# A hybrid decoder layer: the scores' first product with half the key columns, and the states' products placed right behind the scores

## The chip, the cores and the metric

The kernel runs on one core of one Trainium2 chip. The metric is the device time of one execution in microseconds (us). Before the change it is 824.81 us, the median of three runs (824.79 to 825.79 us). The differences in this case are small, so times are given to a hundredth.

## The reference

One layer with two token mixers side by side, then a gated feed-forward part, on 512 tokens of 1024 channels in float32. The change touches one of the mixers, the chunked gated linear attention with 4 heads, 128 key channels and 256 value channels per head, and chunks of 64 tokens:

```
b = jnp.cumsum(gk, axis=3)
q_dec = q * jnp.exp(b)
k_inv = k * jnp.exp(-b)
k_end = k * jnp.exp(b_last - b)
causal = jnp.tril(jnp.ones((GLA_CHUNK, GLA_CHUNK), dtype=bool))
att = jnp.einsum("bhnid,bhnjd->bhnij", q_dec, k_inv)
att = jnp.where(causal, att, 0.0)
o_intra = jnp.einsum("bhnij,bhnjv->bhniv", att, v)
kv_chunk = jnp.einsum("bhnjd,bhnjv->bhndv", k_end, v)
...
return dec[..., None] * state + kv, state
...
o_inter = jnp.einsum("bhnid,bhndv->bhniv", q_dec, s_prev)
o = o_intra + o_inter
```

`att` are the scores, `kv_chunk` the products from which the running state is made, and `o` adds what comes from the scores and what comes from the state.

## The kernel before

The kernel joins two chunks of 64 tokens into one block of 128, so a head has four blocks (`NT` = 4, the loop index `p`). Tiles are 128 partitions by 512 elements. Large projections are made in `col_tile`: eight steps of three matmuls each (lines 448, 449, 450, in a form of 32-bit floats that is split in a high and a low part), 24 matmuls with 512 moving columns. The attention's own small products are plain float32 matmuls, and each of these is two passes on TensorE in the profile, so 4 calls are 8 rows of the trace.

The loop at lines 1228 to 1244 runs five times and overlaps two heads. In one turn the order in the source is: decays and queries of the new head; `scores` of the head before (`old`), and inside it the gated outputs of the head before that; keys of the new head; `states` of `old`; one projection `gate_r`; `outputs` of `old`; a second `gate_r`. In the last turn there is no new head, and the projections are those of `gate_b`. The text below calls the four times that a head's scores are made the first to the fourth head.

What the steps do, with their lines:

- `scores` (1020): four transposes of the decayed keys into one PSUM bank (1024); a copy of that bank to SBUF as `kt` on ScalarE (1026); between them the other head's gated transposes (1080) and their VectorE work (1083); then, into one bank, eight products (1032 and 1033), two for each block `p`; then one predicated copy on VectorE (1034) that writes the allowed scores into the tile `att`, which was set to zero once at the start. The tile `k` of a block holds five stretches of 64 columns, and `flat(k, p, i)` takes two of them, 128 columns, as the stationary operand. Both products have 64 moving columns (queries). In 1032 the second half of the 128 key columns is the later chunk, which the queries of the earlier chunk may not see: `keep` masks it.
- `states` (1038): three products of `kt` with the values (1046), two in one PSUM bank and one in a second, each 256 columns wide; then one copy (1050) and two multiply-adds (1053) on VectorE.
- `outputs` (1056): products of `att` with the values (1065) and of the queries with the states (1067), squares on ScalarE (1069), a sum on VectorE (1071), a power on GpSimd (500), and the scaled outputs on ScalarE (1074).

PSUM has two sets of banks: `mm_bank` takes one of five, `ax_bank` one of three. A bank is given out again when its last reader is done. The transposes, the scores, the states and the outputs use the small set; projections and one half of the gated transposes use the large set.

The order on each engine is not written out in this part. A planner walks through the program with its own estimate of every instruction's time and gives each engine, whenever it is free, the instruction earliest in the source whose inputs are ready by that estimate. The order is then fixed: on the chip each engine takes its instructions in that order and waits where an input is late. Weights are read ahead: `weight` issues loads on SyncE's queue, splits an earlier weight into its parts on ScalarE (385, 387) and VectorE (390), and hands pieces of the convolution (782 on ScalarE, 786, 778, 800 to 804 on VectorE) to the engines, so that these stand between the head's own work on the same queues.

Of the kernel before, what the change touches and what calls it, by code (L numbers as in the profile page):

```python
# [17 lines left out]
P = 128  # L18
D = 1024
T = 512  # L20
NT = T // P
# [54 lines left out]
def trunk_layer(ctx: ExitStack, tc: tile.TileContext, a: dict, out: bass.AP):  # L76
    nc = tc.nc
# [23 lines left out]
    def nm(s):  # L101
        return f"{s}_{next(names)}"

    def heap(dt=F32):
        return hp.tile([P, T], dt, tag="h", name=nm("h"))
# [13 lines left out]
    def mm_bank():  # L119
        return ps.tile([P, T], F32, tag="mm", name=nm("mm"), bufs=5)  # L120

    def ax_bank():
        return ps.tile([P, T], F32, tag="ax", name=nm("ax"), bufs=3)
# [14 lines left out]
    keep = cp.tile([P, P], U8, name="keep")  # L138
    att = gp.tile([P, NT, P], F32, name="att")
# [268 lines left out]
    def weight(name, j, ahead=LOOK):  # L408
        assert order[used[0]] == (name, j)
        prefetch(1)  # L410
        used[0] += 1
        prefetch(ahead)
        share = {"two": 2.5, "w_glu": RATE + 0.75}.get(name, RATE)

        fill(share + (1.75 if order[min(len(ready), len(order)) - 1] in ADDED else 0))
        return ready[used[0] - 1]
# [35 lines left out]
    def col_tile(w, acts, acc=None, lo=0, hi=T, at={}, ks=range(KT)):  # L452

        if acc is None:
            acc = mm_bank()
        for k in ks:
            s = slice(k * P, (k + 1) * P)
            ah, al = acts[k]
            mm3(acc[:, lo:hi], (w[0][:, s], w[1][:, s]), (ah[:, lo:hi], al[:, lo:hi]), k == 0, k == KT - 1)
            if k in at:  # L460
                at[k]()
        return acc
# [89 lines left out]
    start = tc.manual_schedule(engines=START)  # L552
    start.__enter__()
    rows = tp.tile([P, P], F32, tag="gain", name=nm("rows"), bufs=1)[0:KT, :]
# [259 lines left out]
    for k in range(KT):  # L814
# [3 lines left out]
        pa = col_tile(weight("w_glu", 2 * k), acts1)  # L818
        c = heap()
# [104 lines left out]
    rows = slice(32, 32 + RANK)  # L924
# [9 lines left out]
    rows = slice(96, 96 + RANK)  # L934
# [24 lines left out]
    def gl(n, tag, bufs):  # L959
        return gp.tile([P, n], F32, tag=tag, name=nm(tag), bufs=bufs)  # L960
# [3 lines left out]
    C = 64  # L964
# [5 lines left out]
    def flat(t, p, i):  # L970
        return t[:, p, i : i + 2, :].rearrange("p c j -> p (c j)")
# [4 lines left out]
    class Head:  # L976
# [43 lines left out]
        def scores(self, between=None):  # L1020
            q, k = self.q, self.k
            pt = ax_bank()
            for p in range(NT):
                nc.tensor.transpose(pt[:, p * P : (p + 1) * P], flat(k, p, 3), ident)
            self.kt = gl(T, "kt", 1)
            nc.scalar.copy(self.kt, pt)
            if between:
                between()
            pa = ax_bank()
            for p in range(NT):  # L1030
                c = p * P
                nc.tensor.matmul(pa[:, c : c + C], flat(k, p, 0), q[:, p, 0, :], start=True, stop=True)  # L1032
                nc.tensor.matmul(pa[:, c + C : c + P], flat(k, p, 1), q[:, p, 2, :], start=True, stop=True)  # L1033
            nc.vector.copy_predicated(
                att, keep.unsqueeze(1).to_broadcast([P, NT, P]), pa.rearrange("p (a i) -> p a i", a=NT)
            )

        def states(self):

            self.s = [None]  # L1040
            kv = []
            for p in range(NT - 1):
                if p % 2 == 0:
                    pkv = ax_bank()
                kv.append(pkv[:, (p % 2) * DV : (p % 2 + 1) * DV])
                nc.tensor.matmul(kv[p], self.kt[:, p * P : (p + 1) * P], self.v(p), start=True, stop=True)  # L1046
            for p, half in enumerate(kv):
                new = gl(DV, "state", 3)
                if p == 0:
                    nc.vector.tensor_copy(new, half)  # L1050
                else:
                    dec = self.dec[:, p : p + 1]
                    nc.vector.scalar_tensor_tensor(new, self.s[p], dec, half, ALU.mult, ALU.add)
                self.s.append(new)
# [33 lines left out]
    def gate_r(m):  # L1088
        pr = col_tile(weight("w_r", m), acts1)
        sr[m] = heap()  # L1090
        nc.scalar.activation(sr[m], pr, AF.Silu)
# [3 lines left out]
    def gate_b(m):  # L1095
        gbs[m] = col_tile(weight("w_gb", m), acts1)
# [131 lines left out]
    for h in range(HEADS + 1):  # L1228
        old = heads[h - 1] if h else None
        new = heads[h] if h < HEADS else None  # L1230
        if new:
            new.decays()
            new.queries()
        else:
            gate_b(0)
        if old:
            old.scores(heads[h - 2].gated if h > 1 else None)
        new.keys() if new else gate_b(1)
        if old:
            old.states()  # L1240
        gate_r(2 * h) if new else gate_b(2)
        if old:
            old.outputs()
        gate_r(2 * h + 1) if new else gate_b(3)
# [378 lines left out]
    for gi, pairs in enumerate(GROUPS):  # L1623
        acts = []
        if gi == 0:
# [8 lines left out]
            p, q = pairs[0]  # L1634
# [139 lines left out]
```

## Time and profile before

| what | value |
|---|---|
| median of three runs | 824.81 us |
| the profiled execution: its time | 824.81 us |
| the profiled execution: span from first to last instruction | 823.1 us |
| mean granted TensorE clock | 0.998 of full speed |
| the attention's loop in the span | about 168 to 285 us |

How to read the rows of the trace: in the order of time, a row is the start in us, the time it took, the engine, the line, the operation, what it writes and reads, the operands' shapes and the number of instructions joined in the row; in brackets the idle time of the engine just before it and what ended it. PE is TensorE's matmul and PEld its weight load, which runs beside PE; DVE is VectorE, ACT is ScalarE, POOL is GpSimd. Matmuls are pipelined, so a row's length (from issue to the modelled end) is longer than the step to the next row, and the step is what counts for PE. The page's groups by line give a mean in ns and the idle time before.

### The profile page before, as it was taken

The numbers are of one execution on the slowest core, as the hardware profiler recorded it, in microseconds if no ns is written. First come the engines' busy times: TensorE is split into PE (matmuls) and PEld (weight loads), VectorE is DVE, ScalarE is ACT, GpSimd is POOL, SyncE is SP. The second block draws the span as 40 slices with busy tenths as digits, with TensorE's granted clock in tenths as the row PEclk, the third lists the DMA queues.
The fourth block names the chain that finished last, engine by engine and source line by source line (L and its number), as shares of the span: only waits on it lengthen the run. The fifth ranks groups of instructions, "written<-read, shape, count | busy, mean of one in ns | idle before, by whom it ended". The sixth has DMA issues, their size and how long they took to land.

```text
span 823.1 us, 11554 instructions
## 1 busy us (share of the span) xinstructions
PE 814.2 (99%) x4323; PEld 704.3 (86%) x4323; DVE 717.1 (87%) x1161; ACT 449.6 (55%) x666; POOL 149.6 (18%) x133
## 2 busy tenths in 40 slices
PE   8999999999999999999999999999999999999996
PEld 7888888888888889999988898898889988899885
DVE  6689999998989599886788889979975999789896
ACT  6643447656664446684454546556435653466654
POOL 2000010001100213543001000230123301612012
PEclk9999999999999999999999999999999999999999
DMA  8355672563433103323647623146632457234662
GB/s 318 102 130 144 148 192 87 129 154 103 101 105 103 51 30 124 104 78 113 203 117 220 192 77 103 32 170 159 140 136 83 142 138 165 105 103 166 167 129 103
DMA packets 30616, 106.27 MB, mean 129 GB/s; under 512 B 3464, under 2 KB 3600, under 8 KB 30560
## 3 DMA queue, kind: packets, MB, share of 16 engines
q1 hardware_dynamic: 24784, 85.34, 30.3%
q0 software_dynamic: 5760, 20.19, 14.4%
q8 instruction: 34, 0.56, 0.3%
q14 instruction: 22, 0.18, 0.1%
q10 hardware_dynamic: 16, 0.00, 0.0%
HBM read 103.42 MB, written 2.10 MB: 128 GB/s over the span
## 4 chain that ended last, share of the span: by engine, by line
PE 98%; DMA 1%; ACT 0%; DVE 0%; POOL 0%; issue 0%; POOLq 0%; SPq 0%; ACTq 0%
PE mm L448 28%; PE mm L449 28%; PE mm L450 28%; PE mm L662 3%; PE ax L450 2%; PE ax L449 2%; PE ax L448 2%; PE ax L1065 1%; PE ax L1067 1%; PE ax L1046 1%; DMA raw<-in_w_v_dram 1%; PE ax L1033 0%; PE ax L1032 0%; PE ax L529 0%; PE ax L576 0%; PE ax L1080 0%
## 5 line engine op out<-in xcount | busy, mean ns | idle before, releaser
L448 PE MATMUL mm<-uh,wlo 128*128 128x512 f32 (+1 forms) x672 | 244.4, 364 | 0.0
L449 PE MATMUL mm<-ul,whi 128*128 128x512 f32 (+1 forms) x672 | 242.3, 361 | 0.0
L450 PE MATMUL mm<-uh,whi 128*128 128x512 f32 (+1 forms) x672 | 242.0, 360 | 0.0
L450 PEld LDWEIGHTS mm<-uh,whi 128*128 128x128 f32 x672 | 126.8, 189 | 19.4
L448 PEld LDWEIGHTS mm<-uh,wlo 128*128 128x128 f32 x672 | 127.0, 189 | 18.9
L449 PEld LDWEIGHTS mm<-ul,whi 128*128 128x128 f32 x672 | 127.0, 189 | 18.6
L385 ACT CAST whi<-raw 128x1024 fp32r<-128x1024 f32 x86 | 89.8, 1047 | 59.9 <-PE mm L450 33.8
L356 DVE TENSOR_TENSOR wlo<-raw,whi 128x1024 fp32r<-128x1024 f32 x80 | 94.2, 1185 | 24.6 <-ACT whi L355 20.7
L327 POOL TENSOR_TENSOR raw<-raw,raw 128x512 f32<-128x512 f32 x42 | 67.5, 1608 | 212.8 <-DVE wlo L356 117.1
L390 DVE TENSOR_TENSOR wlo<-raw,whi 128x1024 fp32r<-128x1024 f32 x70 | 91.2, 1306 | 16.1 <-ACT whi L385 16.1
L355 ACT CAST whi<-raw 128x1024 fp32r<-128x1024 f32 x80 | 76.3, 957 | 35.9 <-PE mm L450 27.0
L786 DVE SCALAR_TENSOR_TENSOR c<-h,pp,c 128x255 f32<-128x255 f32 (+14 forms) x120 | 56.1, 467 | 3.7 <-ACT c L782 3.4
L786 DVE SCALAR_TENSOR_TENSOR c<-aside,btmp,c 128x255 f32<-128x255 f32 (+14 forms) x120 | 56.1, 467 | 2.8 <-ACT c L782 2.7
L786 DVE SCALAR_TENSOR_TENSOR aside<-h,pp,aside 128x255 f32<-128x255 f32 (+6 forms) x112 | 52.3, 467 | 0.0
L355 ACT CAST whi<-kept 128x1024 fp32r<-128x1024 f32 (+1 forms) x32 | 31.8, 995 | 30.6 <-DVE kept L310 17.1
L1498 DVE SCALAR_TENSOR_TENSOR tmp<-mm,pp,tmp 128x511 f32<-128x511 f32 (+1 forms) x56 | 41.4, 742 | 4.0 <-ACT tmp L1495 3.9
L356 DVE TENSOR_TENSOR wlo<-kept,whi 128x1024 fp32r<-128x1024 f32 (+1 forms) x32 | 36.8, 1153 | 4.8 <-ACT whi L355 4.7
L1176 ACT COPY tmp<-mm 128x256 f32<-128x256 f32 x48 | 17.6, 367 | 34.3 <-PE mm L450 33.9
L1414 DVE TENSOR_TENSOR hres<-hres,mm 128x512 f32<-128x512 f32 (+1 forms) x49 | 32.2, 670 | 4.2 <-PE mm L450 2.7
L1495 ACT ACTIVATE tmp<-mm,pp 128x512 f32<-128x512 f32 x28 | 21.8, 777 | 19.1 <-PE mm L450 18.9
L387 ACT ACTIVATE wlo<-raw 128x1024 fp32r<-128x1024 f32 x16 | 16.8, 1059 | 22.1 <-PE mm L448 22.1
L1498 DVE SCALAR_TENSOR_TENSOR tmp<-tmp,pp,tmp 128x511 f32<-128x511 f32 (+1 forms) x32 | 27.8, 888 | 0.4
(350 smaller groups left out, 1783.5 us busy)
## 6 DMA issues: line engine op xcount, KB each, us to landing
raw<-in_w_up_dram SPq DMA_DIRECT2D x44, 512.0 KB, 3.7
raw<-in_w_glu_dram SPq DMA_DIRECT2D x16, 512.0 KB, 4.8
raw<-in_w_down_dram SPq DMA_DIRECT2D x15, 512.0 KB, 4.1
kept<-in_w_down_dram POOLq DMA_DIRECT2D x10, 512.0 KB, 5.5
raw<-in_w_v_dram SPq DMA_DIRECT2D x8, 512.0 KB, 5.5
raw<-in_w_qk_dram SPq DMA_DIRECT2D x8, 512.0 KB, 3.3
raw<-in_w_r_dram SPq DMA_DIRECT2D x8, 512.0 KB, 4.6
wlo<-in_w_r_dram POOLq DMA_DIRECT2D x8, 512.0 KB, 8.0
```

The costliest lines, as they stand in the source:

```text
L327: work = nc.gpsimd.tensor_tensor(out, x, y, ALU.add)
L355: nc.scalar.copy(hi, raw)
L356: two_low[:] = [nc.vector.tensor_tensor(lo, raw, hi.bitcast(F32), ALU.subtract)]
L385: nc.scalar.copy(hi, raw)
L390: pace[0] = nc.vector.tensor_tensor(lo, raw, hi.bitcast(F32), ALU.subtract)
L448: nc.tensor.matmul(acc, ll, rh, start=first, stop=False, **kw)
L449: nc.tensor.matmul(acc, lh, rl, start=False, stop=False, **kw)
L450: nc.tensor.matmul(acc, lh, rh, start=False, stop=last, **kw)
L662: nc.tensor.matmul(acc, act, ready[k // 2][wi][:, j], start=first, stop=last)
L786: nc.vector.scalar_tensor_tensor(out[:, j:], x[:, : half_t - j], w, out[:, j:], ALU.mult, ALU.add)
L1414: done = nc.vector.tensor_tensor(hres[t, n][:, c], hres[t, n][:, c], acc[:, c], op)
L1498: nc.vector.scalar_tensor_tensor(z[:, s:], acc[:, : T - s], w[j], z[:, s:], ALU.mult, ALU.add)
```

## The change

- The two products of a block are no longer made one after the other. First all four blocks' first product, with 64 key columns as the stationary operand in place of 128, written to the first 64 partitions of the bank; then all four second products, as before.
- The masked copy into `att` becomes two: partitions 0 to 63 with all 128 columns of each block, and partitions 64 to 127 with the last 64 columns. The rest of `att` keeps the zeros of the start.
- In the loop, `states` moves from behind `keys` to right behind `scores`.
- Of the two PSUM banks of `states`, the second is taken from the large set.

```
             pa = ax_bank()
+            pb = pa.rearrange("p (a i) -> p a i", a=NT)
+
             for p in range(NT):
-                c = p * P
-                nc.tensor.matmul(pa[:, c : c + C], flat(k, p, 0), q[:, p, 0, :], start=True, stop=True)
-                nc.tensor.matmul(pa[:, c + C : c + P], flat(k, p, 1), q[:, p, 2, :], start=True, stop=True)
-            nc.vector.copy_predicated(
-                att, keep.unsqueeze(1).to_broadcast([P, NT, P]), pa.rearrange("p (a i) -> p a i", a=NT)
-            )
+                nc.tensor.matmul(pb[:C, p, :C], k[:, p, 0, :], q[:, p, 0, :], start=True, stop=True)
+            for p in range(NT):
+                nc.tensor.matmul(pb[:, p, C:], flat(k, p, 1), q[:, p, 2, :], start=True, stop=True)
+            for rows, cols in ((slice(0, C), slice(0, P)), (slice(C, P), slice(C, P))):
+                visible = keep[rows, cols].unsqueeze(1).to_broadcast([C, NT, cols.stop - cols.start])
+                nc.vector.copy_predicated(att[rows, :, cols], visible, pb[rows, :, cols])
...
                 if p % 2 == 0:
-                    pkv = ax_bank()
+                    pkv = mm_bank() if p else ax_bank()
...
             old.scores(heads[h - 2].gated if h > 1 else None)
+            old.states()
         new.keys() if new else gate_b(1)
-        if old:
-            old.states()
         gate_r(2 * h) if new else gate_b(2)
```

## The prediction

> **What bounds the kernel now.** I read the page first, then the busy time by stretch, then the timeline around each of the four places where a head's scores are made. The first five lines are the page's, the next two the busy time by stretch (start and end; then for each engine busy us and instructions; granted clock, DMA share, GB/s).
>
> ```profile
> span 823.1 us, 11554 instructions
> ...
> PE 814.2 (99%) x4323; PEld 704.3 (86%) x4323; DVE 717.1 (87%) x1161; ACT 449.6 (55%) x666; POOL 149.6 (18%) x133
> ...
> PE 98%; DMA 1%; ACT 0%; DVE 0%; POOL 0%; issue 0%; POOLq 0%; SPq 0%; ACTq 0%
> ```
>
> ```profile
> 176.00:203.00 27.00, 27.00 (x127) 22.63 (x126) 26.73 (x62) 13.40 (x24) 2.86 (x2) 1.00 0.49 124
> 168.00:300.00 132.00, 132.00 (x643) 111.77 (x643) 117.39 (x245) 72.82 (x125) 14.45 (x13) 1.00 0.36 96
> ```
>
> The reader is to see that TensorE is the bound, and in the attention's loop without any gap: busy 132.00 of 132.00 us. So a TensorE step that is saved there is won, and a wait that is put into its queue is lost in full. VectorE is nearly as full (117.39, and 26.73 of 27.00 between the first two heads' scores).
>
> The order of one turn, on the first head:
>
> ```profile
> 173.49 0.60 PE L1024 MATMUL ax<-ident,k 128*128 128x128 f32 x4
> 173.93 0.33 PE L1032 MATMUL ax<-q,k 128*128 128x64 f32 x2
> ...
> 175.64 0.47 PE L448 MATMUL mm<-uh,wlo 128*128 128x512 f32 x1
> ...
> 181.21 1.46 PE L1046 MATMUL ax<-h,kt 128*128 128x256 f32 x6
> ...
> 182.31 0.58 PE L448 MATMUL mm<-uh,wlo 128*128 128x512 f32 x1
> ...
> 184.72 0.68 DVE L1015 TENSOR_TENSOR k<-mm,tmp 128x512 f32<-128x512 f32 x1
> ```
>
> Transposes, scores (173.93 to 175.64: 1.71 us for 16 passes, 0.107 each), 5.6 us of keys, states, next projection: TensorE keeps the source's order. The keys stand between the transposes and the states, and that is the cover for the copy `kt` that the states read.
>
> **The copy `kt` against the end of the scores.** In each pair below one row is the weight load with which TensorE leaves the scores, the other ScalarE's copy, for the heads 1 to 4.
>
> ```profile
> 175.61 0.19 PEld L448 LDWEIGHTS mm<-uh,wlo 128*128 128x128 f32 x1
> ...
> 176.80 0.57 ACT L1026 COPY kt<-ax 128x512 f32<-128x512 f32 x1
> ...
> 204.89 0.19 PEld L448 LDWEIGHTS mm<-uh,wlo 128*128 128x128 f32 x1
> ...
> 207.41 0.58 ACT L1026 COPY kt<-ax 128x512 f32<-128x512 f32 x1
> ...
> 234.14 0.19 PEld L448 LDWEIGHTS mm<-uh,wlo 128*128 128x128 f32 x1
> ...
> 235.74 0.57 ACT L1026 COPY kt<-ax 128x512 f32<-128x512 f32 x1
> ...
> 261.56 0.58 ACT L1026 COPY kt<-ax 128x512 f32<-128x512 f32 x1
> ...
> 263.40 0.19 PEld L448 LDWEIGHTS mm<-uh,wlo 128*128 128x128 f32 x1
> ```
>
> The copy ends at 177.37, 207.99, 236.31 and 262.14: 1.76, 3.10 and 2.17 us after the scores in heads 1 to 3, and 1.26 before their end in head 4. Today nobody notices. With the states right behind the scores TensorE stands until the copy is there, and with it all that is queued behind: keys, both projections, the outputs.
>
> **What is late before the copy, and does it move?** For head 2, followed backwards from its outputs:
>
> ```profile
> 192.58 1.28 ACT L992 ACT_TABLE_LOAD   x1
> 194.25 1.22 DVE L990 TENSOR_TENSOR_SCAN b<-run,h 128x512 f32<-128x512 bf16 x1
> ...
> 195.50 0.64 ACT L992 ACTIVATE tmp<-b 128x512 f32<-128x512 f32 x1 [1.64 <-DVE b L990]
> 196.04 0.36 ACT L1069 ACTIVATE junk<-ax 128x256 bf16<-128x256 f32 x1
> ...
> 197.99 0.16 DVE L1071 TENSOR_SCALAR mean<-ss 128x4 f32<-128x4 f32 x1
> ...
> 198.24 2.00 POOL L500 TENSOR_TENSOR rstd<-mean,mhalf 128x4 f32<-128x4 f32 x1 [4.78 <-DVE mean L1071]
> ...
> 200.27 1.57 ACT L1074 ACTIVATE o<-ax,rstd 128x256 f32<-128x256 f32 x4 [2.77 <-POOL rstd L500]
> ```
>
> ScalarE takes `kt` behind the scaled outputs (1074), these wait for GpSimd's power, that for VectorE's sum (1071), that for the last square (1069), which stands on ScalarE behind an exponential (992) that waited 1.64 us for VectorE's scan (990). So it is VectorE's full queue that sets the time of head 2's copy, not TensorE. When TensorE loses 1.76 us in head 1, this chain does not follow: the squares before the table load move, but the load then ends at about 192.58 + 1.76 + 1.28 = 195.6, still when the scan is done. Heads 1 and 2 therefore do not add up: TensorE can't pass 207.99 whatever it lost before, a shift of **3.10 in all** by head 2.
>
> Head 3:
>
> ```profile
> 222.18 0.19 ACT L1069 ACTIVATION_READ_ACCUMULATOR junk<-ax 128x1 f32 x1
> ...
> 225.67 0.16 DVE L1071 TENSOR_SCALAR mean<-ss 128x4 f32<-128x4 f32 x1
> ```
>
> The sum came 3.30 after the last square, on VectorE's account again. TensorE and the squares 3.5 later use that up; the copy moves by some 0.8 (VectorE's added work, below) to 237.1, and the scores now end at 234.14 + 3.5 = 237.6 less what they save. No wait is left, barely. In head 4 the copy keeps its 1.26.
>
> **The change part by part.**
>
> *Half the key columns.* Eight of a head's 16 passes get 64 stationary columns for 128. No row has that shape. What the step of a pass hangs on, these rows tell:
>
> ```profile
> 337.09 0.95 PE L840 MATMUL ax<-ones,btmp 128*128 128x1 f32 x8
> 337.91 0.37 PE L448 MATMUL mm<-uh,wlo 128*128 128x256 f32 x1
> ...
> L1032 PE MATMUL ax<-q,k x32: 222/275/275, 173.9 to 263.1; 128*128 128x64 f32 x32
> ...
> L1034 DVE COPY_PREDICATED att<-keep,ax x4: 725/734/753, 178.7 to 264.3; 128x512 f32<-128x512 uint8 x4
> ...
> L1050 DVE COPY state<-ax x4: 415/416/418, 185.9 to 270.8; 128x256 f32<-128x256 f32 x4
> ```
>
> With one moving column the step is 0.82 / 8 = 0.1025, with 64 it is 0.107: moving columns hardly matter; it is the load of 128 columns, or a floor under each pass. If the load, halving saves 8 x 0.053 = 0.43 us a head; if a floor, nothing. Against that stands the change to another array shape and back, twice a head: if the array must first run empty, each costs a pass's length beyond its step, 0.275 - 0.107 = 0.17, so 0.34. The bounds are 0.43 saved and 0.34 lost; I take **0.25 saved**, since the step looks like a load and the drain may be partly hidden. In heads 1 and 2 it is worth nothing, for the copy sets the end there; in heads 3 and 4 it counts: 0.5.
>
> The Trainium skill, "TensorE: Matmul & The Clock Gate", section "LDWEIGHTS (loading the stationary operand)", has the load's time as columns over 1.2 GHz, 107 ns for 128 and 53 for 64. The step of 107 ns agrees for 128; by this rule alone an estimate of the sum below is 3.5 - 0.86 = 2.6. The Trainium skill, "TensorEngine Tiling (Array Packing)", section "Key Properties", says that a change of tiling mode, not just of tile, drains TensorE. It speaks against this change, no run here shows it, and with the drain at the price of the rows an estimate of the sum would be 3.5 - 2 x 0.09 = 3.3.
>
> *Two masked copies.* The first has the columns of today's (0.73 us), the second half of them, near the 0.416 of the 256-column copy: **0.4 us a head more on VectorE**. It is off TensorE's path, but ahead of the scan and the sum that lead to the next copy: head 2's moves from 207.99 to 208.4, and the shift from 3.1 to **3.5**. If the extra meets an idle stretch of VectorE it costs nothing.
>
> *States ahead of the keys.* Six passes move; none is added, and they issue no DMA. The weight loads and splits that the keys' call issues now follow three short VectorE operations (1050, 1053) in the source, on queues with a wait already. The keys come 1.1 us later, plus the wait; their reader on VectorE (1015) is at 184.72, 3.5 us after the keys' last product (before 181.21), which covers 1.1 + 1.76. If not, VectorE loses its lead and the second rival comes nearer.
>
> *A bank of the large set.* Head 2, with readers of three banks:
>
> ```profile
> 202.79 0.68 DVE L1008 SCALAR_TENSOR_TENSOR q<-mm,tmp 128x512 f32<-128x512 f32 x1
> 203.15 0.60 ACT L1091 ACTIVATE h<-mm 128x512 f32<-128x512 f32 x1
> ...
> 209.58 0.74 DVE L1083 SCALAR_TENSOR_TENSOR tmp<-ax,pp,h 128x512 f32<-128x512 f32 x1
> ```
>
> From the small set the third state product would have to wait for the gated half's reader, until 210.32. The large set's two last projections have been read by 203.75, before the scores end, so I cost this at nothing.
>
> **Sum.** 3.10 + 0.4 - 0.5 = **3.0 us**, on the profiled execution's 824.81 us (span 823.1 and 1.7 around it), which is the median: **827.8**. Its own range: 3.1 - 0.86 = 2.2 to 3.5 + 0.68 = 4.2, so 827.0 to 829.0.
>
> **The rivals.**
>
> *No wait (the other side).* The planner gives TensorE what its estimate holds ready. If it holds `kt` unready when the scores end, the keys go first and cover the copy; from 1.76 and 3.10 us of keys on (8 and 14 products of 0.23) the wait is gone, as it is if ScalarE takes the copy earlier. For it: head 4, where the copy is in time. Against: the copy follows the transposes by one instruction in the source, so an estimate without VectorE's lag has it ready. Then only the products count, four heads: from 1.7 faster to 1.4 slower, with 0.25 each 1.0 faster: 823.8.
>
> *Every head waits in full.* If the chain follows TensorE (VectorE's lead eaten up, or another order on ScalarE), the three gaps add up: 1.76 + 3.10 + 2.17 - 0.25 = 6.8, 831.6. Against it: head 2's chain above.
>
> *Narrow passes are dear.* If each waits for the one before (0.275 for 0.107), a head loses 8 x 0.168 + 0.34 = 1.7; head 1 hides it in its wait and head 2 too, heads 3 and 4 pay: 3.5 + 3.4 = 6.9, 831.7. Against it: loads run beside the products today.
>
> **How the numbers follow.** Forecast 0.59, no wait 0.24, every head in full 0.10, dear passes 0.07. The range 823.8 to 831.6 cuts about half of each rival, 0.20. From no change this measurement tells about 0.2%, 1.65 us. Faster by more needs no wait and nearly the whole 1.7: 0.09. Within: the rest of that rival, 0.15. Slower: 0.76.
>
> **What would show it.** TensorE idle before 1046, put down to ScalarE's 1026, some 2 us in head 1 and again in head 2, little or none in 3 and 4; first products with a step well under 0.107, perhaps a gap where their row begins and ends; a second masked copy of about 0.4; no idle time of VectorE before the second head's scan (990). Wrong: no idle before 1046 (then the order or the copy's place differs), or idle before it in head 3 as well.

## The result, and the profile after

The changed kernel takes 828.88 us (828.55 to 829.57, six runs) against 824.80 us (824.56 to 825.79, six runs) of the kernel before on the same chip: a ratio of 1.0046, interval 1.0035 to 1.0056. The forecast was 827.8 us, with a range of its own from 827.0 to 829.0 us.

The page of the changed kernel, its span and the engines' busy time; then TensorE's waits (what waited for what: us in all, times, the longest); then the busy time by stretch, in the columns of the prediction:

```profile
span 826.8 us, 11559 instructions
...
PE 816.6 (99%) x4323; PEld 705.8 (85%) x4323; DVE 720.2 (87%) x1165; ACT 450.0 (54%) x666; POOL 149.6 (18%) x133
```

```profile
PE ax L1048 <- ACT kt L1026: 2.1, 2, 1.6
PE mm L568 <- DVE ones L541: 1.1, 1, 1.1
```

```profile
168.00:303.70 135.70, 133.57 (x643) 111.89 (x642) 120.49 (x249) 73.06 (x125) 14.44 (x13) 0.99 0.36 94
...
175.00:178.00 3.00, 1.39 (x10) 1.20 (x9) 3.00 (x11) 2.05 (x3) 0.00 (x0) 1.00 0.97 172
178.00:181.00 3.00, 3.00 (x9) 2.39 (x8) 2.92 (x7) 0.00 (x0) 0.00 (x0) 0.50 0.69 218
181.00:184.00 3.00, 3.00 (x13) 2.40 (x12) 3.00 (x9) 0.00 (x0) 0.00 (x0) 0.93 0.03 11
184.00:187.00 3.00, 3.00 (x15) 2.48 (x14) 3.00 (x6) 0.93 (x1) 0.00 (x0) 1.00 0.00 0
```

The span grew by 3.7 us, from 823.1 to 826.8, and the attention's loop, which had no gap before, now has 135.70 - 133.57 = 2.13 us without TensorE: two waits for `kt`. That is not all of the 3.7. The rest stands in a column that was 1.00 throughout before: behind the first wait the granted clock is 0.50 for three microseconds and 0.93 for the next three, and TensorE does 9 and 13 instructions there instead of 15.

The timeline of TensorE behind the first head's scores shows both losses:

```profile
177.31 1.42 PE L1048 MATMUL ax<-h,kt 128*128 128x256 f32 x4 [1.61 <-ACT kt L1026]
178.52 1.06 PE L1048 MATMUL mm<-h,kt 128*128 128x256 f32 x2
...
180.23 0.63 PE L450 MATMUL mm<-uh,whi 128*128 128x512 f32 x1
180.66 0.63 PE L448 MATMUL mm<-uh,wlo 128*128 128x512 f32 x1
...
181.48 0.39 PE L450 MATMUL mm<-uh,whi 128*128 128x512 f32 x1
181.72 0.39 PE L448 MATMUL mm<-uh,wlo 128*128 128x512 f32 x1
```

After a wait of 1.61 us, products of 512 columns follow one another by 0.43 us (180.23 to 180.66) instead of 0.23, until about 181.4. The transposes of the second head, which stood at 201.90 before, stand at 205.20: 3.30 us later, of which 1.6 are the wait and 1.7 the half clock.

In the other heads, the same timeline shows the copy and then the states' products of heads 2, 3 and 4:

```profile
208.22 0.57 ACT L1026 COPY kt<-ax 128x512 f32<-128x512 f32 x1
...
208.84 1.13 PE L1048 MATMUL ax<-h,kt 128*128 128x256 f32 x4 [0.52 <-ACT kt L1026]
...
236.81 0.56 ACT L1026 COPY kt<-ax 128x512 f32<-128x512 f32 x1
...
238.03 1.08 PE L1048 MATMUL ax<-h,kt 128*128 128x256 f32 x4
...
265.37 0.58 ACT L1026 COPY kt<-ax 128x512 f32<-128x512 f32 x1
...
267.17 1.08 PE L1048 MATMUL ax<-h,kt 128*128 128x256 f32 x4
```

Head 2 waits 0.52 us, heads 3 and 4 not at all: their copies end at 237.37 and 265.95, 0.66 and 1.22 us before the states begin. From head 3 on nothing more is lost. Its transposes stand 3.93 us later than before (235.08 against 231.15), and the span ends 3.7 us later.

The scores themselves, first as pieces of the chain of waits (start, us, what), then rows of the timeline in stretches cut so that one or all eight passes are joined in a row, then the group of the masked copy:

```profile
236.55 0.61 PE ax L1033 x8
237.16 1.03 PE ax L1035 x8
238.19 0.92 PE ax L1048 x4
```

```profile
236.48 0.27 PE L1033 MATMUL ax<-q,k 128*64 128x64 f32 x1
...
236.48 0.68 PE L1033 MATMUL ax<-q,k 128*64 128x64 f32 x8
...
237.09 0.32 PE L1035 MATMUL ax<-q,k 128*128 128x64 f32 x1
...
237.09 1.10 PE L1035 MATMUL ax<-q,k 128*128 128x64 f32 x8
```

```profile
L1038 DVE COPY_PREDICATED att<-keep,ax x8: 445/581/732, 178.6 to 268.7; 64x512 f32<-64x512 uint8 x4, 64x256 f32<-64x256 uint8 x4
```

One pass alone takes 0.27, eight end after 0.68, so narrow passes follow by 0.41 / 7 = 0.058 us; for the wide ones it is 0.78 / 7 = 0.111. Half the columns is half the step. But eight narrow passes hold the chain for 0.61 us where 8 x 0.058 = 0.47, and eight wide ones for 1.03 where 8 x 0.111 = 0.89: some 0.15 us goes at each of the two changes of shape. Together the scores take 1.64 us (236.55 to 238.19) instead of 1.73 (in the chain before they went from 232.62 to 234.35): 0.09 us saved per head.

### The profile page after: what moved, and what is told of

It is laid out like the page before. It is cut to its first block, busy times and chain, and to the rows that moved or that the text cites. A ratio compares the mean times of both kernels' runs of the same rounds, so it can differ in the third digit from the quotient of the medians.

```text
span 826.8 us, 11559 instructions
## 1 busy us (share of the span) xinstructions
PE 816.6 (99%) x4323; PEld 705.8 (85%) x4323; DVE 720.2 (87%) x1165; ACT 450.0 (54%) x666; POOL 149.6 (18%) x133
## 4 chain that ended last, share of the span: by engine, by line
PE 76%; ACT 1%; POOL 0%; DVE 0%; issue 0%; POOLq 0%; ACTq 0%
PE mm L448 22%; PE mm L449 22%; PE mm L450 22%; PE ax L449 2%; PE ax L450 2%; PE ax L448 2%; PE ax L1067 1%; PE ax L1069 1%; PE ax L1048 1%; PE ax L529 0%; PE mm L1048 0%; PE ax L1035 0%; PE ax L1082 0%; ACT o L1076 0%; POOL rstd L500 0%; ACT L997 0%
```

## The experiments

All spans below are of the profiled execution and are compared with 823.1 us of the kernel before. "Waits" are TensorE's idle times before the states' products of heads 1, 2 and 3.

| kernel | waits, us | half clock in that execution | span | median, us (runs) | ratio to before |
|---|---|---|---|---|---|
| the whole change | 1.61, 0.52, 0 | after head 1 | +3.7 | 828.88 (6) | 1.0046 |
| half_only | none | no | -0.4 | 825.17 (11) | 0.9994 |
| move_only | 1.58, 0.67, 0 | no | +3.1 | 827.91 (5) | 1.0032 |
| head1_only | 1.61, 0, 0 | no | +1.8 | 828.23 (7) | 1.0029 |
| head1_fill | filled, 0, 0 | no | +1.5 | 826.79 (11) | 1.0019 |
| head2_only | 0, 2.28, 0 | after head 2 | +3.7 | 828.96 (5) | 1.0046 |
| in_keys2 | 0.22, 0.32, 0 | no | +0.5 | 825.58 (11) | 1.0004 |
| in_keys4 | none | no | -0.3 | 824.60 (11) | 0.9992 |
| all_fill1 | filled, 2.41, 0 | after head 2 | +5.6 | 831.07 (5) | 1.0071 |
| small_bank | 1.34, 0.64, 0 | no | +2.3 | 827.92 (9) | 1.0025 |
| all_fill12 | filled, 0.37, 1.95 | after head 3 | +7.8 | 833.25 (4) | 1.0090 |
| wide_keys4 | none | no | +0.4 | 825.93 (11) | 1.0006 |

The kernel before read 825.24 us on the chip of the first four experiments, 825.11 on that of the next four and 825.40 on that of the last three; the ratios go by these.

### One part alone: half_only and move_only

half_only is the changed kernel with the states put back:

```
             old.scores(heads[h - 2].gated if h > 1 else None)
-            old.states()
         new.keys() if new else gate_b(1)
+        if old:
+            old.states()
```

> The changed kernel with the states back behind the keys: half the key columns, grouped products, two masked copies and the bank of the large set stay. Theory (the whole loss is the wait for the copy kt and what TensorE's clock does after it): no idle before the states, a scores block of 1.64 us for 1.73, so 0.09 saved in each of four heads: 824.4. Rival A (the narrow array shape costs): 825.5 or more. Rival B (the second masked copy on VectorE delays the chain): up to 4 x 0.44 more, 826.5.

Measured: 825.17 us, ratio 0.9994 (0.9985 to 1.0002), no wait. The interval holds the 0.09 us x 4 = 0.36 us of gain that the chain shows (0.9996) and excludes the prediction's bound of 0.34 us lost in each head (1.0016) and both rivals (825.5 and 826.5 us at a before of 824.8, or 1.0008 and 1.0021).

move_only is the kernel before with the states moved and one bank from the large set, and the full-width products:

```
-                    pkv = ax_bank()
+                    pkv = mm_bank() if p else ax_bank()
...
             old.scores(heads[h - 2].gated if h > 1 else None)
+            old.states()
         new.keys() if new else gate_b(1)
-        if old:
-            old.states()
```

> The kernel before with only the states moved right behind the scores, their second bank from the large set; scores with 128 key columns and one masked copy. Theory: idle of about 1.7 us before the states of head 1, granted clock at half for some 3 us after it, a short idle in head 2, and 4 x 0.09 not saved: 828.9 to 829.3, no faster than the whole change. Rival A (narrow shape): 825. Rival B (second masked copy): 2 us under the whole change, about 827.

Measured: 827.91 us, ratio 1.0032 (1.0019 to 1.0045). At a before of 824.8 that is 827.4: 1.5 us under the theory and near rival B's 827. The profiled execution waits 1.58 and 0.67 us and keeps its clock; of its 3.1 us, 0.5 had come up before the first head (its transposes stand at 173.98 instead of 173.49). The two executions at clock 0.996 of the five (828.77 and 828.89) lie with the whole change. So the move alone carries most of the loss. A share of the second masked copy, by way of head 2's `kt`, is not excluded: with a single masked copy `kt` of head 2 ends at 207.97 here, and at 208.79 in the whole change, but the orders of VectorE and ScalarE differ as well. Without the move the second copy costs nothing that shows (half_only).

### The first head alone: head1_only and head1_fill

The states behind the scores in head 1, behind the keys in the others; then the same with TensorE kept busy by products of ones into a bank that nobody reads:

```
             old.scores(heads[h - 2].gated if h > 1 else None)
+            if h in (1,):
+                filler = mm_bank()
+                for _ in range(7):
+                    nc.tensor.matmul(filler[:, :P], ones, ones, start=True, stop=True)
-            old.states()
+                old.states()
         new.keys() if new else gate_b(1)
+        if old and h not in (1,):
+            old.states()
```

(head1_only is without the three lines of the filler.)

> The changed kernel with the states right behind the scores in head 1 alone, behind the keys in heads 2 to 4. Theory: 1.7 us of idle in head 1, then the clock at half for about 3 us, which costs 1.6 more; no other idle; 4 x 0.09 saved: 824.8 + 3.3 - 0.4 = 827.7. Rival (the clock costs nothing, heads 1 and 2 each pay their own wait): 824.8 + 1.7 - 0.4 = 826.1.

> As the run with head 1 alone, and ahead of head 1's states seven 128-column products of ones into a bank that nobody reads, 14 passes of 0.11 us, so that TensorE works through most of the wait. The wait itself stays. Theory: the clock stays at full, so 1.6 us come back: 826.1. Rival (the clock does not follow the idle): 827.7, as without the products.

Measured: 828.23 us and 826.79 us. The seven runs of head1_only spread over 2.5 us, and the mean granted clock of each sorts them in the main: four at 0.995 and 0.996 took 828.23 to 828.71 us, three at 0.997 to 0.999 took 826.25, 826.58 and 827.78. (By an estimate, some 3.4 us at half clock, as in the whole change, lower the mean over 825 us by 0.002.) The profiled run is the one of 826.58 us, and its stretch behind the wait shows the clock at full:

```profile
175.00:178.00 3.00, 1.39 (x10) 1.17 (x9) 3.00 (x11) 2.05 (x3) 0.00 (x0) 1.00 1.01 176
178.00:181.00 3.00, 3.00 (x15) 2.48 (x14) 2.92 (x8) 0.00 (x0) 0.00 (x0) 1.00 0.63 212
```

The same wait as in the whole change, 1.61 us, and 15 instructions behind it at full clock instead of 9 at half. This execution costs the wait alone, +1.8 us of span; the four at the lower clock have spans of 826.5 to 827.0, some 1.6 to 2.1 us more. With the filler all eleven runs read a clock of 0.997 or more, the wait's time stays lost, and the median falls by 1.4 us, though the intervals of the two ratios (1.0018 to 1.0041 and 1.0010 to 1.0028) overlap. So the half clock is a second loss behind a wait, in some executions and not in others. It is not the only spread: the run of 827.78 us has a clock of 0.999, and the kernel before reads 824.64 to 827.13 us on this chip at 0.997 to 0.999.

The prediction's claim that VectorE's queue, not TensorE, sets head 2's copy can be read in head1_only too (ScalarE's timeline):

```profile
194.12 1.28 ACT L992 ACT_TABLE_LOAD   x1
...
195.99 0.64 ACT L992 ACTIVATE tmp<-b 128x512 f32<-128x512 f32 x1 [0.58 <-DVE b L990]
...
207.91 0.57 ACT L1026 COPY kt<-ax 128x512 f32<-128x512 f32 x1
```

TensorE is 1.55 us late here (its second transposes stand at 203.45 instead of 201.90), and so is the table load; the exponential still waits 0.58 us for the scan, and the copy ends at 208.48, 0.49 us later than before. The scan and the sum stand at 194.73 and 198.48, 0.48 and 0.49 us later than before, so the whole shift is VectorE's. The forecast for that case was 208.4.

### The second head alone: head2_only

As head1_only, with `h in (2,)`.

> The changed kernel with the states' products right behind the scores in head 2 alone; heads 1, 3 and 4 as before, narrow first products everywhere. Times for a before of 824.8 us. If each head pays the whole distance from the end of its scores to its kt (the prediction's bound: in head 2 3.10 us before the change, and in the run with the narrow products alone kt ended 2.2 us after the scores), TensorE stands idle 2.2 to 3.5 us in head 2 and the time is 826.7 to 828.0 us, near the whole change without any wait in head 1, since the waits of heads 1 and 2 do not add up; up to 1.6 us more in executions in which the granted clock falls to a half after the wait. Rival (waits add up head by head, and head 2 costs only the 0.52 us that it shows in the whole change): 825.2 us.

Measured: 828.96 us, ratio 1.0046 (1.0032 to 1.0060): the whole change's time from one head. Its busy time by stretch:

```profile
205.00:208.00 3.00, 0.87 (x2) 0.79 (x3) 3.00 (x8) 3.00 (x6) 0.00 (x0) 0.83 0.00 0
208.00:211.00 3.00, 3.00 (x9) 2.38 (x9) 3.00 (x7) 3.00 (x6) 0.91 (x1) 0.60 0.58 178
```

The wait is 2.28 us and the half clock comes with it; with its 1.6 us the theory reaches the measured time. The rival (825.2 us) falls: what head 2 shows in the whole change, 0.52 us, is only what head 1 had not used up already. The wait is shorter than the 3.1 us of the prediction because the copy ends at 207.07 and not at 207.99: in this kernel's order VectorE takes the sum (1073) ahead of the next head's operations, as it does in half_only (at 196.99, against 197.99 before).

### Work put ahead of the wait: in_keys2, in_keys4, wide_keys4

The states go into the next key projection, behind 2 or 4 of its 8 steps (6 or 12 products of 512 columns):

```
-            old.states()
-        new.keys() if new else gate_b(1)
+        at = {1: old.states} if old else {}
+        new.keys(at) if new else gate_b(1, at)
```

(in_keys4 and wide_keys4 have `3` for `1`; `keys` and `gate_b` hand `at` on to `col_tile`, which calls it behind that step. wide_keys4 is the kernel before with this and with the bank of move_only.)

> The whole change, but the states' products stand behind the first 2 of the 8 steps of the next key projection (6 products of 512 columns, 1.36 us by 0.227 us each) instead of directly behind the scores. Theory (the wait is for kt's copy alone, so work put ahead shortens it one for one): idle before head 1's states 0.3 to 0.5 us instead of 1.61, before head 2's about 1.5 to 2; 826.3 to 827.0 us at a before of 824.8, and 1.6 us more where the clock falls after head 2's wait. Rival (the loss lies in the states' products themselves, their bank or the narrow products): as the whole change, 828.6 us.

> The same with 4 of the 8 key steps ahead (12 products, 2.72 us). Theory: no idle before head 1's states, 0 to 1 us before head 2's; 824.4 to 825.5 us at a before of 824.8. Rival: 828.6 us.

> The kernel before, with its full-width first products, but the states' products moved up to behind the fourth of the eight key steps and one of their banks from the large set. Theory (with 2.72 us of key products ahead no state waits; what the narrow products save is 0.09 us per head of TensorE, 0.36 in all): no idle ahead of the states; 824.8 to 825.2 us at a before of 825.1, 0.2 to 0.6 us above the same order with the narrow products (824.60). Rival (the earlier states are a gain of their own, through VectorE or the outputs): 824.6 us or less, level with the narrow ones.

Measured: 825.58, 824.60 and 825.93 us; ratios 1.0004 (0.9995 to 1.0013), 0.9992 (0.9983 to 1.0001) and 1.0006 (0.9997 to 1.0015). TensorE in in_keys2, heads 1 and 2:

```profile
177.13 1.13 PE L1048 MATMUL ax<-h,kt 128*128 128x256 f32 x4 [0.22 <-ACT kt L1026]
...
206.91 1.13 PE L1048 MATMUL ax<-h,kt 128*128 128x256 f32 x4 [0.32 <-ACT kt L1026]
```

Six products of 0.23 us took 1.4 of the 1.61 us away in head 1, as expected; in head 2 the wait came out at 0.32 instead of 1.5 to 2, since here too the sum stands early and the copy ends at 206.85. So the time came out below the 826.3 to 827.0 us that the theory had (825.1 at a before of 824.8). Twelve products leave no wait and no loss. So the whole price of the change is the missing cover, not the states' products, their bank or the narrow passes. wide_keys4 came out higher than its theory (825.1 to 825.5 at a before of 825.4), and 0.0014 or 1.2 us above in_keys4, where 0.36 was expected from the narrow passes; the sign is right, but the two intervals overlap, so the size stays open. in_keys4 has the lowest ratio of all, yet its interval reaches past 1: it is not told apart from the kernel before.

### Does the half clock of head 1 cost anything in the whole change? all_fill1, all_fill12

The whole change with the filler of head1_fill ahead of head 1's states; then with nine more such products ahead of head 2's.

> The whole change with seven products of ones (128 x 128, into a bank that nobody reads) ahead of head 1's states, so that TensorE is not idle there and its granted clock stays full. Theory (in the whole change head 2's kt sets the end, and what head 1 loses to the half clock head 2 would have waited anyway): the wait before head 2's states grows from 0.52 to about 1.5 to 2.2 us and the time stays at 828 to 829 us, at most 0.7 us below the whole change. Rival (the half clock after head 1's wait is a loss of its own): 1.5 to 1.7 us below the whole change, 827.0 us.

> The whole change with seven products of ones ahead of head 1's states and nine ahead of head 2's (into a bank that nobody reads), so that TensorE is idle for at most 0.3 us in either place. Theory (a wait of about 1.6 us or more costs itself, and then in many executions another 1.6 to 1.7 us of half clock; with head 1 filled, the half clock fell behind head 2): the granted clock stays full and the time is 1.5 to 1.8 us below the kernel with head 1 alone filled, 829.3 us at a before of 825.1, at or a little above the whole change. Rival (the waits alone make the time, the clock's half rate covers only work that waited anyway): as with head 1 alone filled, 831 us.

Measured: 831.07 and 833.25 us. Both theories missed both times. all_fill1 does show what its theory said of the wait: with the clock full behind head 1, TensorE comes to head 2 earlier and waits longer there, 2.41 us where 1.5 to 2.2 were expected (TensorE's timeline):

```profile
209.07 1.13 PE L1048 MATMUL ax<-h,kt 128*128 128x256 f32 x4 [2.41 <-ACT kt L1026]
```

But that wait is then followed by a half clock of its own, and the time rises by 0.0025 or 2.1 us instead of staying. all_fill12 has its clock at 1.00 behind heads 1 and 2, and loses the same thing in head 3 (TensorE's timeline, the busy time by stretch, VectorE's timeline):

```profile
240.45 1.55 PE L1048 MATMUL ax<-h,kt 128*128 128x256 f32 x4 [1.95 <-ACT kt L1026]
```

```profile
241.00:244.00 3.00, 3.00 (x9) 2.37 (x8) 2.96 (x6) 1.24 (x2) 0.00 (x0) 0.50 0.83 137
```

```profile
230.43 0.42 DVE L800 TENSOR_TENSOR c<-c,aside 128x256 f32<-128x256 f32 x1
230.77 0.16 DVE L1073 TENSOR_SCALAR mean<-ss 128x4 f32<-128x4 f32 x1
```

These two kernels test less cleanly than meant. The planner sees the added products too, and writes another order behind them: head 3's sum stands behind more of the convolution's pieces, at 230.77, where the whole change has it at 226.73, and the copy ends at 240.40 instead of 237.37. What they do show is that every wait of 1.95 us and more met in a profiled execution here was followed by the half clock, those of 1.3 to 1.6 us in one of four profiled executions, and those of 0.2 to 0.7 us in none. What the half clock behind head 1 costs in the whole change they leave open. One of the six runs of the whole change, 829.18 us, has a mean clock of 0.999, which by the estimate above leaves no room for such a stretch, and it is no shorter than the others; that speaks for a small cost, but it is a single run.

### The bank: small_bank

```
-                    pkv = mm_bank() if p else ax_bank()
+                    pkv = ax_bank()
```

> The changed kernel with all three of the states' products of a head in banks of the small set, as before the change. The order that the planner then writes puts one key product ahead of head 1's states, and in head 2 eight key products between the second and the third states' product; heads 3 and 4 stand as in the whole change. Theory (the bank costs nothing by itself, and in the small set the third product would only come later): the wait before head 1's states 1.4 us, before head 2's as in the whole change, the third product of head 2 about 1.8 us after the second, no further wait; 827.5 to 829.3 us at a before of 824.8. Rival (the bank of the large set is what delays the key products or the outputs): at least 1 us below the whole change and no wait in head 2, 826 us.

Measured: 827.92 us, ratio 1.0025 (1.0016 to 1.0035). At a before of 824.8 that is 826.9, between the theory's range and the rival's 826, and by the ratios 1.7 us below the whole change. But the rival's sign, no wait in head 2, is not there: the waits are 1.34 and 0.64 us. The profiled execution keeps its clock. TensorE and VectorE in head 2:

```profile
207.07 1.13 PE L1048 MATMUL ax<-h,kt 128*128 128x256 f32 x4 [0.64 <-ACT kt L1026]
...
209.67 0.40 PE L449 MATMUL mm<-ul,whi 128*128 128x512 f32 x1
210.10 0.70 PE L1048 MATMUL ax<-h,kt 128*128 128x256 f32 x2
```

```profile
209.31 0.74 DVE L1085 SCALAR_TENSOR_TENSOR tmp<-ax,pp,h 128x512 f32<-128x512 f32 x1
```

The third product starts 0.05 us after the gated half's reader ends (210.05); eight key products stand in between, so TensorE does not idle for it. The bank of the large set removes that dependence, and no wait for a bank shows in the whole change. That the small set comes out lower goes with the order that the planner writes for it: one key product ahead of head 1's states, and an early sum (196.97), so that head 2's copy ends at 207.02 and not at 208.79. The bank and the order that follows from it were not tried apart.

## Why the prediction was right, and where its sizes were off

**The bound and the place of the loss: right.** TensorE as the bound (816.6 of 826.8 us busy), the copy `kt` without its cover, waits of 1.61 us in head 1 and 0.52 in head 2 (some 2 were forecast for each), none in 3 and 4. half_only and move_only put the loss on the move, and in_keys2 and in_keys4 take it away by work put ahead.

**Heads 1 and 2 don't add up: right for the step, as far as the order holds.** head1_only moves TensorE by 1.55 us and head 2's copy by 0.49, with 0.4 forecast; head2_only alone costs as much as the whole change. But the position of the sum on VectorE, on which this rests, is not a constant. In the kernels of this study head 2's copy ends at 206.85 to 209.11, according to where the planner puts the sum (ahead of the next head's operations, between them, or behind the second scan) and how many of the weights' splits (385, 387) ScalarE takes ahead of the copy.

**Head 2's copy at 208.4, a shift of 3.5: under-sized.** It ended at 208.79, 0.80 us later than before, a shift of 3.9. The larger part is VectorE's own queue: the scan stands at 194.81 instead of 194.25, 0.56 us later, where 0.4 was forecast. The rest is the half clock. The prediction let TensorE be 1.76 us late and left a margin up to the scan; with the half clock TensorE was 3.3 us late, and the late squares delayed the exponential (ScalarE's timeline, then VectorE's):

```profile
195.65 0.21 ACT L1071 ACTIVATION_READ_ACCUMULATOR junk<-ax 128x1 f32 x1
195.87 1.28 ACT L992 ACT_TABLE_LOAD   x1
197.17 0.63 ACT L992 ACTIVATE tmp<-b 128x512 f32<-128x512 f32 x1
```

```profile
194.81 1.23 DVE L990 TENSOR_TENSOR_SCAN b<-run,h 128x512 f32<-128x512 bf16 x1
...
197.27 0.43 DVE L804 TENSOR_TENSOR c<-c,aside 128x255 f32<-128x255 f32 x1
...
197.83 0.17 DVE L1000 COPY ea<-tmp 128x4 f32<-128x4 f32 x1
...
198.79 0.17 DVE L1073 TENSOR_SCALAR mean<-ss 128x4 f32<-128x4 f32 x1
```

The exponential (197.17) no longer waits for the scan. It ends at 197.80, and VectorE's copy that reads it (1000) begins at 197.83, 0.56 us behind the operation before it, where the kernel before has 0.33 (196.71 to 197.04). That is the other 0.23 us of the sum's 0.80 (197.99 to 198.79).

The half clock behind a wait is a term that the prediction had not, but of the 1.7 us that TensorE lost to it only these 0.2 or so reached head 2's copy. TensorE was ready for head 2's states at 208.32; at full clock, by an estimate from these rows, it would have been at 206.6 and waited some 2 us for the copy, as forecast. So most of the half clock stands in place of head 2's wait, which was 0.52 us. That it cost so little was luck: behind head 2's wait, where head2_only and all_fill1 have it, no later wait takes it up.

**0.25 us a head saved by the narrow products: 0.09 measured.** Both sides of the prediction's term came true at once, each a little under its bound: the step halves (0.058 against 0.11 us a pass; the bound was 0.43 saved) and each change of shape costs about 0.15 (the bound was 0.34 lost). By the Trainium skill, "TensorE: Matmul & The Clock Gate", section "LDWEIGHTS (loading the stationary operand)", 64 columns load in 53 ns, with which 0.058 agrees. By the Trainium skill, "TensorEngine Tiling (Array Packing)", section "Key Properties", a change of tiling mode drains TensorE. It gives no price; a loss of 0.15 us at each change of shape is in line with it. Heads 3 and 4 give back 0.2 us instead of 0.5, and that is what the ends show: 3.9 - 0.2 = 3.7.

**The second masked copy, 0.4 us: 0.445 for its own row, 0.59 in VectorE's queue.** The pair holds the queue from 178.56 to 179.76, 1.20 us, where the single copy held it from 178.71 to 179.32, 0.61 us (VectorE in the whole change, then in the kernel before):

```profile
178.56 1.17 DVE L1038 COPY_PREDICATED att<-keep,ax 64x512 f32<-64x512 uint8 x2
179.76 0.42 DVE L1052 COPY state<-ax 128x256 f32<-128x256 f32 x1
```

```profile
178.71 0.72 DVE L1034 COPY_PREDICATED att<-keep,ax 128x512 f32<-128x512 uint8 x1
179.32 0.47 DVE L786 SCALAR_TENSOR_TENSOR c<-h,pp,c 128x249 f32<-128x249 f32 x1
```

in_keys4 with the pair and wide_keys4 with the single copy show the same (1.23 and 0.62 us), and head 2's scan at 194.97 and 194.23. What the pair alone does to head 2's copy was not tried.

**The bank at no cost: right** as far as waits go, down to the reader that the third product would have waited for.

**Sum.** 3.5 - 0.5 = 3.0 forecast, 3.9 - 0.2 = 3.7 in the span. The medians differ by 4.1; the profiled execution itself took 828.60 us, 0.3 below its median, and the six lie within 1.0 of each other.

**The rivals.** No wait: it did not happen; had it, its time would have been that of half_only or in_keys4, by the ratios 0.5 to 0.7 us below before, which is not told apart from no change, and not 1.0, for the same mis-sized 0.25. Every head in full (831.6) and dear passes (831.7) did not happen. all_fill12 shows that the first is near: with another order head 3 waits as well.

## What to carry to other kernels

Where an engine is full, the order of its queue hides latencies that no wait shows; before work is moved out of such a gap, compare for each turn when the operand is ready with when the engine would be, and put as much other work ahead as the worst turn lacks (12 products here; 6 were nearly enough). Price a wait on TensorE at more than its length: add what the clock may do behind it. And where a planner sets the order, an edit in one head moves others, so that a difference of a microsecond between two variants may be the order's and not the edit's.

## What was not expected of the hardware

A wait of TensorE of 1.61 us was followed by a granted clock of 0.50, a loss of 1.7 us more, in the profiled execution of the whole change and, by their mean clocks, in four of seven runs of head1_only; in the profiled execution of head1_only the same wait cost only itself. With waits of 2.28, 2.41 and 1.95 us it came in each profiled execution. By the granted clock in stretches of 0.2 us it lasted 3.4 us in all four: from 178.0 to 181.4 in the whole change, 207.0 to 210.4 in head2_only, 210.5 to 213.9 in all_fill1 and 241.0 to 244.4 in all_fill12. Its start is not tied to the wait: it comes 0.1 us before the wait's end in head2_only, and 0.6, 0.7 and 1.4 us after it in all_fill12, the whole change and all_fill1.

The Trainium skill, "TensorE: Matmul & The Clock Gate", section "Part 1: The HAM clock gate", has the clock fall to half after a whole idle window of about 3.4 us, and rise again after a busy one, in a window that runs on by itself. The length agrees. The condition does not: the waits here were half to seven tenths of such a window. A window that runs on by itself would fit a start that is not tied to the wait and a wait that costs differently from run to run; no run here shows the window itself, and what decides it was not tried and stays open.
